# A step rule and a rate for the second instruction stream of a hybrid decoder block

## The chip, the core and the metric

The kernel runs on one core of a Trainium2 chip. The core has a matrix engine (TensorE, PE), a vector engine (VectorE, DVE), a scalar engine (ScalarE, ACT), a general engine (GpSimd, POOL), a queue engine (SyncE, SP) and 16 DMA engines. Each engine takes its instructions from one queue, in the order in which the program was built. The metric is the device time of one execution in microseconds (us), lower being better.

## What is computed

The reference is one decoder block on 1024 tokens of width 1024. Its parts, shortened:

```
h  = x * (1 + scale1) + shift1                     # scale, shift, gate from c (w_ada)
q, k, v, z, xbc, dt, g = split(h @ w_in)
y_attn = diff_attention(q, k, v) @ w_attn_branch   # 8 heads, causal
y_ssd  = mamba2(z, xbc, dt) @ w_ssd_branch         # 32 heads, chunks of 256
mixed  = (sig(g1) * y_attn + sig(g2) * y_ssd) @ w_out
x  = layer_norm(ALPHA * x + gate1 * mixed)
h2 = x * (1 + scale2) + shift2
# PEER, per token: 8 heads pick 16 of 16384 experts each (128 per token)
sc = q_j . sub_keys ; eidx, g = top 16 of the 16 x 16 sums of the best keys
act  = gelu(expert_u[eidx] . h2)
y    = sum(softmax(g) * act * expert_v[eidx])
x  = layer_norm(ALPHA * x + gate2 * y)
```

## The kernel before

**Work.** The tokens are worked in two halves of 512 (`hb` 0 and 1), and each half in four tiles of 128. `main` goes through both halves: attention, the state-space mixer (`ssd`), the output projection with its norm (`post_norm`), and the scores of the expert keys (`scores`). These are the main phases. Then `dense` begins.

**Experts in two ways.** Tiles 1, 2 and 3 are done densely: `dense` goes through all 128 blocks of 128 experts (product `ps_u`, GELU, a table of gates, product `ps_v`). For it, `spread` has to build those tables first: per token a one-hot matrix `first_k` on DVE and one, `second_k`, on POOL, and their product `ps_gate` on PE (128 of each for one tile). Tiles 0 and 4 to 7 are done by gathering (`gathered`): 128 indirect DMAs of 512 KB from `peer_u`, each reduced on DVE (line 1130), then a transposition `ps_wT`, then 128 indirect DMAs from `peer_v`, whose rows PE multiplies with `own` into `ps_y` (a copy on DVE at line 1158 for every four rows). At its end `finish` adds the residual and the last norm (lines 1205 to 1217). Both kinds need `route` first, which finds the experts of a tile on DVE.

**Two streams.** The main stream is `main` and then `dense`. Beside it runs the other stream, of two parts: `side` (the modulation's rest, then the gathers of one tile after another) and `urgent` (the routing of one tile after another, with `spread` where the tile is dense). After each step of the main stream, `drive` adds its cost times `ratio` (`ratio1` in `dense`) to a credit and takes steps of the other stream until it is spent; `step` decides whether a step goes to `side` or `urgent`, by a count and the pair `share` (first number in the main phases, second in `dense`).

**What sets the order on the engines.** A scheduler lays out each engine's queue when the program is built. Instructions of the main stream, and the other stream's matmuls (`inline`), have the same high priority and go by program order among themselves when they are ready by the scheduler's own estimate; the rest of the other stream fills gaps. POOL's instructions of the other stream keep program order. `behind` keeps the other stream on DVE and SP from running ahead of the main stream.

**Buffers that tie the streams.** In the main phases the gathers have four buffers (`n_grow`), ten in `dense`. One bank of PSUM (`gate`) serves `ps_gate`, `ps_wT` and `ps_y`; `claim` hands it over. Four buffers of the tag `row` go round in program order among `scr`, `oh`, `gs`, `ys`, `gy`, the loads of `finish`, and the loads `lnr` of `rows_out`. `rows_out` (lines 991 to 1000), called by `scores`, is the last user of the norm's tiles `v`, whose memory `dense` takes over for `act_t`.

Of the kernel before, what the change touches and what calls it, by code (L numbers as in the profile page):

```python
# [47 lines left out]
class Block:  # L48
# [4 lines left out]

    lead = 2
    ahead = 1000000
    ratio = 0.9
    ratio1 = 1.1

    share = 1, 4
    lag = 6, 2  # L60

    behind_by = 2
# [1325 lines left out]
    def step(self, only=None):  # L1388

        insts = self.nc.cur_bb.bb.instructions  # L1390
        n = len(insts)
        forced = only is not None
        if not forced:
            self.count += 1
            turn = self.count % (1 + self.share[self.dp is not None])
            only = "urgent" if turn == 0 or not self.side else "side"
            if only == "urgent" and (not self.urgent or self.claimed == "side"):
                only = "side"
        order = [only] if forced else [only, "side" if only == "urgent" else "urgent"]
        for which in order:  # L1400
            cost = None
            if which == "urgent" and self.urgent:
                cost = next(self.urgent, None)
                if cost is None:
                    self.urgent = None
            elif which == "side" and self.side:
                cost = next(self.side[0], None)
                if cost is None:
                    self.side.popleft()

            if cost:
                break
        for i in insts[n:]:
            if self.after.get(i.engine):
                self.behind(i, self.after[i.engine])
            if i.engine == mybir.EngineType.Pool:
                if self.pool:
                    self.behind(i, self.pool)
                self.pool = i.name
        return max(cost or 0.0, 0.6)  # L1420
# [123 lines left out]
```

## Time and profile before

| | us |
|---|---|
| three runs | 4841.60, 4845.84, 4854.27; median 4845.84 |
| the profiled execution | 4879.04, span 4877.3 |
| main phases (first half; second half) | to about 1102; to about 2489 |
| entry to `dense` (PE between first and second block) | 2493.9 to 2655.3 |
| `dense` | 2655.3 to about 4445 |
| gathers of tile 7 after it | about 4445 to 4877 |

The profiled execution is 33 us (0.7%) longer than the median of the three runs; differences are worked out in its times. Engines: PE is busy in 82% of the span, DVE in 61%, POOL in 38%, ACT in 29%.

In a row of the timeline the first number is the start and the second the duration, both in us; a bracket gives the time that the engine was idle before, and what ended that. In a row of the windows view a stretch and its length are followed by the busy time of each engine with its count of instructions, then the granted clock of TensorE, the busy share of the DMA engines and their GB/s. A gather's row on POOL is the issuing, not the transfer.

### The profile page before, as it was taken

The page shows a single profiled execution, that of the slowest core. Times are in us where ns is not written, and L with a number is a line of the kernel's source. Part 1 is how long each engine was busy: PE and PEld are TensorE (multiplying, and loading weights), DVE is VectorE, ACT ScalarE, POOL GpSimd, SP SyncE. Part 2 cuts the span into 40 slices and gives each one's busy share as a digit, 9 for nine tenths or more (in the row PEclk, how much of TensorE's full clock was granted, in tenths as well). Part 3 has the DMA queues.
Part 4 walks back from the last instruction along what each step waited for, and adds up shares of the span by engine and source line. Part 5 has one row for each costly group of instructions (what it writes and reads, how often), then busy time and mean ns, then how long its engine had stood idle before and what let it go on. Part 6 is the DMA issues. An engine that isn't in the chain of part 4 may idle for free.

```text
span 4877.3 us, 52557 instructions
## 1 busy us (share of the span) xinstructions
PE 4001.2 (82%) x17996; PEld 2769.0 (57%) x17996; DVE 2976.9 (61%) x6965; ACT 1419.5 (29%) x2340; POOL 1862.1 (38%) x1704
## 2 busy tenths in 40 slices
PE   6999999998888878999975768997799976994045
PEld 4677667786667756755554655556655665552000
DVE  6664646558887896744356994228952399324920
ACT  3544444323453343631112221222222222210000
POOL 1000000001266435333333565445654376445764
PEclk9999999998898988999975989998899989997588
DMA  7323233443356736478744898888988899888998
GB/s 261 121 70 117 76 106 111 146 145 119 95 166 187 245 116 179 115 251 279 257 121 142 325 330 333 298 313 329 370 313 316 313 363 330 309 292 284 395 357 315
DMA packets 441343, 1135.18 MB, mean 233 GB/s; under 512 B 141596, under 2 KB 162228, under 8 KB 441076
## 3 DMA queue, kind: packets, MB, share of 16 engines
q0 software_dynamic: 188704, 677.46, 39.0%
q1 hardware_dynamic: 126644, 405.04, 24.3%
q10 hardware_dynamic: 125728, 49.32, 3.8%
q8 instruction: 143, 2.34, 0.2%
q14 instruction: 124, 1.02, 0.1%
HBM read 1067.56 MB, written 64.11 MB: 232 GB/s over the span
## 4 chain that ended last, share of the span: by engine, by line
PE 52%; DVE 22%; DMA 9%; issue 8%; POOL 6%; ACT 2%; SPq 0%; ACTq 0%; POOLq 0%; DVEq 0%
PE ps_y L1300 9%; DVE grow L1130 7%; PE ps_u L269 7%; PE ps_v L1340 6%; PE ps_b L269 5%; DMA grow<-in_peer_u,ei 4%; PE ps_x L269 4%; DVE wlo L220 3%; PE ps_z L269 3%; PE ps_g L269 3%; POOL grow L1188 3%; PE ps_pq L269 3%; POOL second_k L1272 3%; PE ps_vT L269 2%; PE ps_o L269 2%
## 5 line engine op out<-in xcount | busy, mean ns | idle before, releaser
L1188 POOL DMA_INDIRECT grow<-in_peer_u,ei x640 | 834.0, 1303 | 765.4 <-DVE ei L1233 199.8
L1188 POOL DMA_INDIRECT grow<-in_peer_v,ej x640 | 679.8, 1062 | 766.1 <-PE ps_y L1300 642.4
L219 ACT CAST whi<-wraw 128x1024 fp32r<-128x1024 f32 x498 | 518.1, 1046 | 1228.3 <-PE ps_u L269 401.5
L220 DVE TENSOR_TENSOR wlo<-wraw,whi 128x1024 fp32r<-128x1024 f32 x498 | 606.2, 1219 | 406.2 <-ACT whi L219 361.0
L1130 DVE SCALAR_TENSOR_TENSOR grow<-grow,gh 128x1024 f32<-128x1024 f32 x640 | 766.7, 1218 | 107.7 <-DMA grow<-in_peer_u,ei 104.0
L1300 PE MATMUL ps_y<-grow,own 128*32 128x512 f32 x2560 | 580.7, 620 | 67.8 <-issue 28.7
L1272 POOL TENSOR_SCALAR second_k<-iota_c,at 128x128 f32<-128x128 f32 x384 | 321.7, 847 | 493.0 <-PE ps_gate L1300 303.8
L269 PE MATMUL ps_u<-hhi,wlo 128*128 128x384 f32 x1024 | 383.6, 375 | 138.3 <-DVE wlo L220 138.3
L269 PE MATMUL ps_u<-hhi,whi 128*128 128x384 f32 x1024 | 378.9, 370 | 66.6 <-ACT act_t L1314 52.5
L269 PE MATMUL ps_u<-hlo,whi 128*128 128x384 f32 x1024 | 370.2, 362 | 0.0
L975 POOL DMA_DIRECT2D h2s_d<-bighi x8 | 4.5, 564 | 914.9 <-ACT bighi L245 914.9
L269 PEld LDWEIGHTS ps_u<-hhi,wlo 128*128 128x128 f32 x1024 | 212.4, 207 | 215.2 <-DVE wlo L220 162.5
L1158 DVE COPY own<-wt 128x4 f32<-128x4 f32 x160 | 28.8, 182 | 433.9 <-PE ps_y L1300 342.6
L269 PEld LDWEIGHTS ps_u<-hhi,whi 128*128 128x128 f32 x1024 | 212.6, 208 | 133.6 <-ACT act_t L1314 63.5
L1340 PE MATMUL ps_v<-wlo,ehi 128*128 128x512 f32 x768 | 259.5, 414 | 34.2 <-DVE wlo L220 34.0
L1300 PEld LDWEIGHTS ps_y<-grow,own 128*32 128x32 f32 x2560 | 88.1, 110 | 326.0 <-issue 200.6
L1340 PE MATMUL ps_v<-whi,ehi 128*128 128x512 f32 x768 | 216.8, 405 | 41.6 <-ACT whi L219 38.9
L1340 PE MATMUL ps_v<-whi,elo 128*128 128x512 f32 x768 | 250.7, 404 | 0.0
L1300 PE MATMUL ps_gate<-first_k,second_k 128*128 128x128 f32 x768 | 176.4, 360 | 85.8 <-POOL second_k L1272 59.1
L269 PEld LDWEIGHTS ps_u<-hlo,whi 128*128 128x128 f32 x1024 | 211.8, 207 | 22.4 <-issue 19.3
L1300 PEld LDWEIGHTS ps_gate<-first_k,second_k 128*128 128x128 f32 x768 | 142.3, 246 | 128.9 <-POOL second_k L1272 93.8
L1340 PEld LDWEIGHTS ps_v<-wlo,ehi 128*128 128x128 f32 x768 | 142.0, 193 | 118.6 <-DVE wlo L220 51.2
(340 smaller groups left out, 7996.0 us busy)
## 6 DMA issues: line engine op xcount, KB each, us to landing
wraw<-in_w_in SPq DMA_DIRECT2D x160, 512.0 KB
wraw<-in_peer_uT SPq DMA_DIRECT2D x128, 512.0 KB
wraw<-in_peer_v SPq DMA_DIRECT2D x128, 512.0 KB
wada<-in_w_adaT SPq DMA_DIRECT2D x48, 512.0 KB
g_d<-gs ACTq DMA_DIRECT2D x48, 512.0 KB
gl<-g_d SPq DMA_DIRECT2D x48, 512.0 KB
cr<-cum_d SPq DMA_DIRECT2D x64, 256.0 KB
wraw<-in_w_ssd SPq DMA_DIRECT2D x32, 512.0 KB
```

Of the source, the lines that this page charges most:

```text
L219: nc.scalar.copy(hi, raw)
L220: i = nc.vector.tensor_tensor(lo, raw, hi.bitcast(F32), op=ALU.subtract)
L269: i = self.nc.tensor.matmul(ps, w[x][:, k, :], r[y][:, k, :], start=k + n == 0, stop=k == kk - 1 and n == 2)
L975: nc.gpsimd.dma_start(self.h2s_d[part][:, k, :], big[k][part][:, P * self.few[0] :])
L1130: nc.vector.scalar_tensor_tensor(u, u, 1.0, h2, op0=ALU.mult, op1=ALU.mult, accum_out=act[:, k : k + 1])
L1158: nc.vector.tensor_copy(own[:, :, OWN - 1].rearrange("p (h r) -> p h r", h=2), wt[:, b * n : b * n + n].rearrange("p (h r) -> p h r", h=2) ...
L1188: self.nc.gpsimd.indirect_dma_start(out=r, out_offset=None, in_=table, in_offset=bass.IndirectOffsetOnAxis(ap=ei[:, k : k + 1], axis=0),)
L1272: nc.gpsimd.tensor_scalar(second, self.iota_c, at[:, 1, k : k + 1], None, op0=ALU.is_equal)
L1300: return op(*args, **kw)
L1340: nc.tensor.matmul(acc[2 * tt + c], prev[x][:, tt * P : tt * P + P], v[y].rearrange("p k c -> p (k c)")[:, c * 512 : c * 512 + 512], start ...
```

## The change

Three numbers and one expression. In the main phases the credit grows at 1.25 times the main stream's cost instead of 0.9. There, of every two steps one went to `urgent` and one to `side`; now of three steps two go to `urgent` and one to `side`. In `dense` one step of five goes to `urgent`, before and now, and `ratio1` stays.

```
-    ratio = 0.9
+    ratio = 1.25
     ratio1 = 1.1
 
-    share = 1, 4
+    share = 3, 5
...
-            turn = self.count % (1 + self.share[self.dp is not None])
-            only = "urgent" if turn == 0 or not self.side else "side"
+            turn = self.count % self.share[self.dp is not None] == 0
+            only = "side" if self.side and turn != (self.dp is not None) else "urgent"
```

No instruction is added or removed; the order on the engines changes. PE where `dense` begins, before: `ps_u` is the product of its first blocks, `ps_key` and `ps_gate` belong to the spread of tile 3.

```order
L269 MATMUL ps_u<-hlo,whi 128x384
L269 MATMUL ps_u<-hhi,wlo 128x384
L1300 MATMUL ps_key<-ident,keys 128x128 x2
L1300 MATMUL ps_key<-ident,g 128x128
L1300 MATMUL ps_gate<-first_k,second_k 128x128 x128
L269 MATMUL ps_u<-hhi,whi 128x384
```

Between the first block of `dense` (24 `ps_u`) and the second stand all 128 gate products of tile 3. PE at the same place now:

```order
L269 MATMUL ps_u<-hlo,whi 128x384
L269 MATMUL ps_u<-hhi,wlo 128x384
L1300 MATMUL ps_gate<-first_k,second_k 128x128 x13
L1300 MATMUL ps_wT<-ident,act 128x128
L1300 MATMUL ps_y<-grow,own_101 32x512 x8
L1300 MATMUL ps_y<-grow,own_103 32x512 x8
```

The last row but one and the last alternate, 32 rows of eight, and then the second block follows: of the gate products 13 are left here, and the transposition and all 256 `ps_y` products of tile 0, which stood among the main stream's before, have come here.

POOL around the end of the main phases, before (`peer_v` with `ej` are the second gathers of tile 0; the two loads at line 1009 serve `dense`):

```order
L1272 TENSOR_SCALAR second_k<-iota_c,at 128x128 x68
L1188 DMA grow<-in_peer_v,ej 128x1024 x39
L1009 DMA hlo<-h2s_d_117 128x8x384
L1009 DMA hhi<-h2s_d_116 128x8x384
L1188 DMA grow<-in_peer_v,ej 128x1024 x85
L1272 TENSOR_SCALAR second_k<-iota_c,at 128x128 x128
```

The last 124 of the second gathers stand ahead of the one-hot matrices of tile 3. The same now, up to the first gathers of tile 4:

```order
L1272 TENSOR_SCALAR second_k<-iota_c,at 128x128 x4
L1188 DMA grow<-in_peer_u,ei 128x1024
L1272 TENSOR_SCALAR second_k<-iota_c,at 128x128 x4
L1188 DMA grow<-in_peer_u,ei 128x1024 x3
L1188 DMA grow<-in_peer_v,ej 128x1024 x128
L1188 DMA grow<-in_peer_u,ei 128x1024 x128
```

The one-hot matrices of tile 3 stand among the first gathers of tile 0, four to one, and all 128 second gathers come behind the last of both.

## Rows read from the trace of the kernel before

**Rows 1.** The page: busy times, and one costly group of part 5.

```profile
PE 4001.2 (82%) x17996; PEld 2769.0 (57%) x17996; DVE 2976.9 (61%) x6965; ACT 1419.5 (29%) x2340; POOL 1862.1 (38%) x1704
...
L1130 DVE SCALAR_TENSOR_TENSOR grow<-grow,gh 128x1024 f32<-128x1024 f32 x640 | 766.7, 1218 | 107.7 <-DMA grow<-in_peer_u,ei 104.0
```

**Rows 2.** Windows: PE, PEld, DVE, ACT, POOL busy, in four stretches.

```profile
771.88:1102.50 330.62, 312.21 (x1479) 252.71 (x1478) 180.85 (x360) 113.51 (x168) 8.70 (x16) 0.97 0.44 142
1518.87:2075.90 557.03, 483.96 (x2323) 381.78 (x2322) 427.17 (x972) 251.14 (x396) 240.80 (x244) 0.89 0.56 169
2075.90:2489.10 413.20, 396.77 (x1784) 226.44 (x1783) 177.38 (x496) 88.92 (x125) 134.87 (x127) 0.98 0.76 254
2493.85:2655.30 161.45, 77.58 (x260) 60.01 (x259) 89.78 (x249) 37.70 (x36) 78.11 (x128) 0.51 0.39 105
```

**Rows 3.** Timeline of PE at the entry to dense.

```profile
2493.51 0.34 PE L269 MATMUL ps_u<-hhi,wlo 128*128 128x384 f32 x1
2507.15 0.80 PE L1300 MATMUL ps_key<-ident,keys 128*128 128x128 f32 x2 [13.30 <-DVE keys L1255]
...
2621.34 2.39 PE L1300 MATMUL ps_gate<-first_k,second_k 128*128 128x128 f32 x8 [1.21 <-POOL second_k L1272]
2655.32 0.69 PE L269 MATMUL ps_u<-hhi,whi 128*128 128x384 f32 x1 [31.59 <-ACT act_t L1314]
```

**Rows 4.** Timeline of ACT: what the first GELU of dense waited for.

```profile
2653.48 1.28 ACT L1314 ACT_TABLE_LOAD   x1 [28.61 <-DMA h_d<-v]
```

**Rows 5.** Timeline of DVE: the start of rows_out.

```profile
2622.41 4.71 DVE L991 TENSOR_TENSOR v<-v,lnr 128x1024 f32<-128x1024 f32 x4
```

**Rows 6.** Windows of tile own alone (PE, PEld, DVE, POOL): the gathers' ps_y.

```profile
2075.90:2489.10 413.20, 124.47 (x512) 17.68 (x512) 5.24 (x30) 0.00 (x0) 0.98 0.76 254
```

**Rows 7.** Windows of tile ps_gate alone (PE, PEld, ACT).

```profile
1518.87:2075.90 557.03, 65.69 (x338) 55.30 (x337) 48.44 (x43) 0.89 0.56 169
```

**Rows 8.** Windows of DVE alone: tile oh, then tile val (route of tile 3).

```profile
2040.00:2507.00 467.00, 22.87 (x24) 0.96 0.71 237
2040.00:2507.00 467.00, 22.02 (x137) 0.96 0.71 237
```

**Rows 9.** Timeline of POOL: gathers, six of tile 0 and one of tile 7.

```profile
1183.66 1.05 POOL L1188 DMA_INDIRECT grow<-in_peer_u,ei  x1 [199.82 <-DVE ei L1233]
...
1887.28 1.00 POOL L1188 DMA_INDIRECT grow<-in_peer_u,ei  x1 [0.17 <-issue]
...
2299.16 0.94 POOL L1188 DMA_INDIRECT grow<-in_peer_v,ej  x1 [0.30 <-issue]
2301.68 1.05 POOL L1188 DMA_INDIRECT grow<-in_peer_v,ej  x1 [1.57 <-PE ps_y L1300]
...
2308.66 0.94 POOL L1188 DMA_INDIRECT grow<-in_peer_v,ej  x1 [0.78 <-PE ps_y L1300]
...
2313.43 0.94 POOL L1188 DMA_INDIRECT grow<-in_peer_v,ej  x1 [2.24 <-DMA grow<-in_peer_v,ej]
...
2322.41 0.94 POOL L1188 DMA_INDIRECT grow<-in_peer_v,ej  x1 [2.28 <-DMA grow<-in_peer_v,ej]
...
4662.57 1.13 POOL L1188 DMA_INDIRECT grow<-in_peer_u,ei  x1 [0.30 <-issue]
```

**Rows 10.** Timeline of PE: ps_y of tile 0, then first and last of tile 7.

```profile
2307.32 1.05 PE L1300 MATMUL ps_y<-grow,own 128*32 128x512 f32 x4 [1.06 <-DMA grow<-in_peer_v,ej]
...
2317.86 1.05 PE L1300 MATMUL ps_y<-grow,own 128*32 128x512 f32 x4 [0.84 <-DMA grow<-in_peer_v,ej]
...
4671.51 4.23 PE L1300 MATMUL ps_y<-grow,own 128*32 128x512 f32 x16 [0.56 <-DVE own L1158]
...
4853.79 1.05 PE L1300 MATMUL ps_y<-grow,own 128*32 128x512 f32 x4 [0.20 <-DMA grow<-in_peer_v,ej]
```

**Rows 11.** Timeline of DVE: finish of tile 7.

```profile
4864.93 1.23 DVE L1205 TENSOR_TENSOR gy<-gy,gr 128x1024 f32<-128x1024 f32 x1 [15.51 <-DMA gr<-x_d]
4866.19 1.23 DVE L1210 SCALAR_TENSOR_TENSOR gy<-gr,gy 128x1024 f32<-128x1024 f32 x1
```

## The prediction

> **What bounds the kernel now.** I read the page first: PE is busy in 82% of the span, DVE in 61%, POOL in 38% [rows 1]. That is an average over stages, so next I read the windows by stage. In the last stretch of the second half (gates of the mixer's output, projection, norm, key scores; 2076 to 2489) PE is busy for 396.77 of 413.20 us, or 96%. In the stretch before it, attention's output and the mixer (1519 to 2076), PE is at 87% and DVE at 77%. At the entry to the dense phase, 161.45 us long, no engine is busy for more than 90 us, and the granted clock is 0.51, about the lower of its two levels [rows 2]. The timeline of PE says what this entry is: PE ends the first dense block at 2493.85, waits 13.30 us for the keys of tile 3, does that tile's gate products until 2623.73, and then waits 31.59 us for a GELU [rows 3]. The GELU waited for a write of `v`, the end of `rows_out` [rows 4], which began at 2622.41 [rows 5], when the spread of tile 3 had given back its buffers. So the entry is serial. Whatever of the other stream stands on PE between the first and the second dense block is paid in full there, and `rows_out` is paid after it.
>
> **What moves, part by part.** The new rate and the new share put the one-hot matrices of tile 3 earlier and the first gathers of tile 0 later. The order shows the result. Of 128 gate products of tile 3, 112 go into the last stretch of the main phases and 16 stay behind the last key scores. All 128 second gathers of tile 0 (512 KB each), their 256 `ps_y`, 32 copies on DVE, the write of `y` and `finish` leave that stretch and come to the entry. PE's queue is in order, so the second dense block stands behind all `ps_y`; everything behind it (GELU, DVE's gate multiplication, the loads of further blocks, whose three buffers are full) waits for it.
>
> *The main phases get shorter.* `ps_y` of the gathers leaves: 124.47 us of PE [rows 6]. The gates that come cost 65.69 / 169 = 0.389 us of PE each (338 records are 169 products) [rows 7], and 112 of them 44 us. PE's busy time in the last stretch becomes 396.8 - 124.5 + 44 = 316 us. How full PE is then is not shown. The first half's stretch of the same work, with none of this beside it, has 312.21 of 330.62 (94%), and the stretch with gates has 87% [rows 2]: 336 or 363 us, against 413. I take 350, a gain of 63 (50 to 77). Route 3 moves the other way, into the mixer's stretch, whose DVE is already at 77%: at least 22.87 + 22.02 = 45 us of DVE [rows 8]. From there 34 reductions of the first gathers leave, 34 x 1.22 = 41 us of DVE [rows 1]. These nearly cancel; I take a cost of 10, between 0 and 45. Together -53 us, between -77 and -5.
>
> *The entry gets longer.* Term by term, from the end of the first dense block:
> The rest of the spread and of the first gathers: 16 gates at the pace of the entry before, (2623.73 - 2507.15) / 128 = 0.91 us [rows 3], are 15 us; six first gathers on POOL, some 7 us at one in 1.2 us, lie partly between them. 18 (15 to 22).
> From the last first gather's issue to the first `ps_y`: 4671.51 - 4662.57 = 9 us in tile 7 [rows 9, 10]; nothing hides it.
> The 128 second gathers. With ten buffers tile 7's `ps_y` last from 4671.51 to 4854.84, 183 us or 1.43 each [rows 10]; that is the lower end. Here there are four. One turn of a buffer is issue to product (2307.32 - 2301.68 = 5.64, or 2317.86 - 2313.43 = 4.43), the product 1.05, and release to the next issue (2308.66 - 2308.37 = 0.29) [rows 9, 10]: 5.8 to 7.0 us, and with four in flight 1.44 to 1.75 each. The stretch with four buffers in which PE most often waited for them runs from 2299.16 to 2322.41, twelve gathers, 1.94 each [rows 9], but there PE also had work of its own. I take 1.75, between the turn's long end and that row: 224 us, and 8 for three hand-overs of the one bank, in which four buffers run empty (an estimate, three product waits of 2 to 3 us): 232. The upper end is 1.94 x 128 + 8 = 256.
> From the last `ps_y` to `rows_out`: tile 7 needed 4864.93 - 4854.84 = 10 us to the first multiplication of `finish`, then 2.5 for two of them [rows 11], which release the buffers of `lnr`; its load takes about as long as one of those before it, 5. 18 (13 to 21).
> From the start of `rows_out` to the second dense block: 2655.32 - 2622.41 = 33 [rows 3, 5].
> Sum 18 + 9 + 232 + 18 + 33 = 310 us, where 161.5 were [rows 2]: +148.5, between +92 and +180.
>
> The trace's 4.43 to 5.64 us from issue to product stand against the fit in the Trainium skill, "DMA: Bandwidth & Descriptors", section "Anatomy of one DMA — SWDGE (gpsimd) path", of 2.0 us plus the bytes over 436 GB/s, which makes 3.2 us of one of these gathers; by that the turn is 4.5 us, POOL's issuing at 1.24 us becomes the limit, the second gathers last an estimated 167 us and the sum would be 65 us less. The rows do not agree with it, and I go by them.
>
> *Dense and after it.* Routes 4 to 7 and their gathers start after `rows_out` as before, the step rule there is unchanged, and on PE 288 `ps_y` stand behind the last dense product where 292 did. So the 2222 us from the second dense block to the end (4877.3 - 2655.3) stay.
>
> *Sum:* +148.5 - 53 = +95.5 us on a span of 4877.3. The profiled execution (4879.04) lies 33 us above the median; I carry the difference over unchanged: 4845.84 + 95.5 = 4941 us. From the ends, 92 - 77 = +15 and 180 - 5 = +175, so 4861 to 5021 for this case.
>
> **Rivals.**
> *The early stretches give back more (faster).* The first gathers of tile 0 ran from 1183.66 to 1887.28, 5.5 us each [rows 9]. If the main stream in attention and mixer went at their pace, 34 fewer of them there give back up to 34 x 5.5 = 187 us, and the time is 4941 - 187 = 4754. It decides the sign from 2.8 us a gather. For it: that stretch is much longer than its work on PE. Against it: over all 640 reductions DVE was idle only 104 us for a landing [rows 1], 0.16 us each, so what slows that stretch is mostly the work itself. 8%.
> *The last stretch does not shrink (slower still).* Gates come in pairs of engines (POOL's matrix, PE's product, ACT's copy out of the one bank), and 112 of them with 28 reductions among a main stream that waits in order may hold it at 413 us; route 3 costs its 45. Then +148.5 + 45 = +194, or 5040. For it: the 87% of the stretch with gates. Against it: DVE has 236 us free in that stretch [rows 2]. 12%.
> *It comes to nothing.* The other stream goes at its own pace, not at the credit's; what the entry loses the main phases give back. That needs the second gathers at 1.43 us and the last stretch at its 336 us, the low end: about +15, or, with a little from the first rival, 4846. 7%.
>
> **How the numbers follow.** My case has 73%, the rivals 8, 12 and 7. About 0.3% (15 us) is what a measurement of this kernel can tell from no change. Slower: 71 of my 73, the 12, and 1: 84%. Within: 2 of mine, 4 of the third rival and 1 of the first: 7%. Faster: 7 of the first rival and 2 of the third: 9%. The range takes my case's low end with a little of the third rival, 4856, and reaches to the second rival, 5040.
>
> **What would show it.** In the profile after: between the first and second dense block PE holds `ps_y` of tile 0, about 230 us of it with PE waiting for gathers (the step's size), and the gap there is near 310 us; `rows_out` follows `finish`; the last key scores end 40 to 70 us earlier than 2489; from the second dense block to the end it is 2222 us give or take 15. I am wrong if the gap is under 220 us, if the key scores end later than before, or if the dense phase or the gathers after it change length by more than 30 us.

## The result, and the profile after

The changed kernel took 4916.3 us (median of three runs, 4905.27 to 4919.57), against 4845.84: the ratio is 1.0137, with a 95% interval of 1.0104 to 1.017. It is slower by 1.4%, 70 us, where 95 had been forecast. The medians of the kernel before lay at 4846, 4847, 4868, 4868 and 4852 us in this set and the four that follow, so kernels of different sets are compared below by their ratio to it; 1% is 48 us.

The windows of the kernel after, by stage: start and end, length, then busy time (and count) of PE, PEld, DVE, ACT and POOL, PE's granted clock, the busy share of the 16 DMA engines, and GB/s. The stages are the first half's mixer, the last stretch of the first half, the second half's attention, its output and mixer, its last stretch, the entry, dense, and what comes after the last dense product.

```profile
331.50:784.10 452.60, 421.82 (x1914) 320.00 (x1913) 244.25 (x435) 196.87 (x335) 0.00 (x0) 0.96 0.29 93
784.10:1117.00 332.90, 310.89 (x1473) 251.58 (x1472) 178.76 (x358) 112.22 (x166) 8.69 (x16) 0.97 0.44 140
1117.00:1516.60 399.60, 363.65 (x1648) 252.39 (x1646) 333.07 (x1060) 188.00 (x376) 119.72 (x117) 0.91 0.33 100
1516.60:2042.50 525.90, 469.18 (x2306) 372.14 (x2305) 405.07 (x959) 244.08 (x385) 214.42 (x229) 0.93 0.53 164
2042.50:2400.10 357.60, 309.37 (x1518) 253.13 (x1517) 258.27 (x640) 119.79 (x156) 140.00 (x149) 0.90 0.56 171
2405.00:2704.40 299.40, 152.86 (x540) 25.66 (x538) 46.61 (x104) 9.80 (x13) 134.73 (x146) 0.83 0.82 277
2704.40:4501.50 1797.10, 1547.16 (x6895) 1056.09 (x6895) 1090.48 (x2372) 390.72 (x537) 963.27 (x775) 0.94 0.88 320
4501.50:4914.20 412.70, 134.34 (x513) 19.72 (x513) 194.86 (x382) 3.50 (x7) 281.02 (x250) 0.70 0.93 357
```

Set these beside [rows 2]: the last stretch fell from 413.20 to 357.60 us, the mixer's from 557.03 to 525.90, and the entry grew from 161.45 to 299.40. Read the last two columns as well. In the last stretch before, PE was 96% busy and the DMA engines were at 0.76 and 254 GB/s; after, that stretch has 0.56 and 171 GB/s, and the entry, where PE works half the time, has 0.82 and 277.

The timeline of PE at the entry (start, length, line, operation; in brackets the idle time before it and what ended it), as in [rows 3]:

```profile
2404.62 0.34 PE L269 MATMUL ps_u<-hhi,wlo 128*128 128x384 f32 x1
...
2416.30 1.96 PE L1300 MATMUL ps_gate<-first_k,second_k 128*128 128x128 f32 x6 [0.50 <-POOL second_k L1272]
2429.14 0.48 PE L1300 MATMUL ps_wT<-ident,act 128*128 128x128 f32 x1 [10.88 <-DVE act L1135]
2430.17 4.87 PE L1300 MATMUL ps_y<-grow,own 128*32 128x512 f32 x16 [0.56 <-DVE own L1158]
...
2659.11 1.05 PE L1300 MATMUL ps_y<-grow,own 128*32 128x512 f32 x4 [0.55 <-DMA grow<-in_peer_v,ej]
2704.36 0.69 PE L269 MATMUL ps_u<-hhi,whi 128*128 128x384 f32 x1 [44.20 <-ACT act_t L1314]
```

The wait for keys of [rows 3] is gone. PE ends the first dense block at 2404.96, works through the last gates, and then through all `ps_y` of tile 0, at the pace at which gathers land. Then it waits 44.20 us for the GELU, as it waited 31.59 before. The timeline of POOL shows the gathers at the ends of that stretch, and the first gather of tile 4:

```profile
2420.12 0.94 POOL L1188 DMA_INDIRECT grow<-in_peer_u,ei  x1 [0.30 <-issue]
2421.37 0.94 POOL L1188 DMA_INDIRECT grow<-in_peer_v,ej  x1 [0.31 <-issue]
...
2653.32 0.94 POOL L1188 DMA_INDIRECT grow<-in_peer_v,ej  x1 [0.34 <-PE ps_y L1300]
...
2772.51 1.39 POOL L1188 DMA_INDIRECT grow<-in_peer_u,ei  x1 [118.25 <-DMA gh<-h_d]
```

The timeline of DVE, with `finish` of tile 0 and the start of `rows_out` (compare [rows 5, 11]):

```profile
2670.65 1.22 DVE L1205 TENSOR_TENSOR gy<-gy,gr 128x1024 f32<-128x1024 f32 x1 [24.12 <-DMA gr<-x_d]
...
2677.56 4.63 DVE L991 TENSOR_TENSOR v<-v,lnr 128x1024 f32<-128x1024 f32 x4 [1.42 <-DMA lnr<-in_ln_g]
```

`rows_out` began 17.4 us after the last `ps_y` (2677.56 - 2660.16) and waited for its row, loaded into a buffer that `finish` had held.

### The profile page after: what moved, and what is told of

Same layout as the page of the kernel before. It is cut to its first block, busy times and chain, and to the rows that moved or that the text cites. A ratio compares the mean times of both kernels' runs of the same rounds, so it can differ in the third digit from the quotient of the medians.

```text
span 4914.2 us, 52631 instructions
## 1 busy us (share of the span) xinstructions
PE 3988.6 (81%) x17996; PEld 2749.0 (56%) x17996; DVE 2972.2 (60%) x6965; ACT 1414.7 (29%) x2338; POOL 1879.1 (38%) x1704
## 4 chain that ended last, share of the span: by engine, by line
PE 27%; DVE 14%; DMA 9%; issue 7%; POOL 3%; ACT 1%; ACTq 0%; POOLq 0%; SPq 0%; DVEq 0%
PE ps_u L269 7%; PE ps_v L1340 7%; PE ps_y L1300 7%; DVE grow L1130 6%; DMA grow<-in_peer_v,ej 5%; DMA grow<-in_peer_u,ei 4%; POOL grow L1188 3%; DVE wlo L220 2%; PE ps_pq L269 1%; PE ps_b L269 1%; PE ps_o L269 1%; PE ps_g L269 1%; PE ps_gate L1300 1%; PE ps_z L269 1%; PE ps_x L269 0%
## 5 line engine op out<-in xcount | busy, mean ns | idle before, releaser
L1188 POOL DMA_INDIRECT grow<-in_peer_u,ei x640 | 859.1, 1342 | 734.9 <-DVE ei L1233 199.7
L1188 POOL DMA_INDIRECT grow<-in_peer_v,ej x640 | 659.1, 1030 | 628.5 <-PE ps_y L1300 503.1
L1300 PE MATMUL ps_y<-grow,own 128*32 128x512 f32 x2560 | 611.9, 622 | 117.2 <-DMA grow<-in_peer_v,ej 98.0
L1272 POOL TENSOR_SCALAR second_k<-iota_c,at 128x128 f32<-128x128 f32 x384 | 334.4, 878 | 669.0 <-PE ps_gate L1300 408.1
L269 PEld LDWEIGHTS ps_u<-hlo,whi 128*128 128x128 f32 x1024 | 207.7, 203 | 19.4 <-issue 16.8
L245 ACT CAST ehi<-act_t 128x384 fp32r<-128x384 f32 x128 | 65.7, 513 | 504.6 <-PE ps_v L1340 500.5
L1314 ACT ACTIVATE act_t<-ps_u 128x384 f32<-128x384 f32 x128 | 62.6, 489 | 499.6 <-PE ps_u L269 456.2
```

The source lines that it names most:

```text
L245: nc.scalar.copy(hi, src)
L269: i = self.nc.tensor.matmul(ps, w[x][:, k, :], r[y][:, k, :], start=k + n == 0, stop=k == kk - 1 and n == 2)
L1188: self.nc.gpsimd.indirect_dma_start(out=r, out_offset=None, in_=table, in_offset=bass.IndirectOffsetOnAxis(ap=ei[:, k : k + 1], axis=0),)
L1272: nc.gpsimd.tensor_scalar(second, self.iota_c, at[:, 1, k : k + 1], None, op0=ALU.is_equal)
L1300: return op(*args, **kw)
L1314: nc.scalar.activation(t, ps[:, :n], AF.Gelu)
```

## The experiments

The 13 profiles are best read side by side. "First dense" is the start of the first dense product, "gap" the time between the first and the second dense block, "tile 4" its first gather, and GB/s the mean from the first dense product to the end.

```
run           ratio   95%             first dense  gap    tile 4   span    GB/s
before again  (before)                2490.7       162    2714.1   4858.3  313
after         1.0137  1.0104-1.0170   2399.8       299    2772.5   4914.2  321
ratio         1.0059  1.0037-1.0080   2504.2       165    2729.8   4858.7  314
share         1.0055  1.0034-1.0076   2354.8       310    2743.2   4867.1  322
lnr_after     1.0082  1.0060-1.0103   2396.8       none   2925.7   4869.2  325
cut           0.9790  0.9755-0.9824   2401.6       145    2624.3   4766.9  321
bufs5         1.0006  0.9993-1.0018   2389.3       269    2736.0   4859.8  327
lnr_before    1.0041  1.0029-1.0053   2490.7       184*   2765.2   4889.8  310
lnr_share32   1.0074  1.0043-1.0105   2369.2       none   2893.7   4890.4  319
share_bufs5   0.9987  0.9976-0.9998   2381.0       268    2724.9   4856.4  326
late_rate     1.0089  1.0072-1.0107   2360.6       310    2748.0   4899.9  319
before_bufs5  0.9910  0.9893-0.9928   2485.7       147    2707.5   4817.3  317
lnr_cut       0.9683  0.9663-0.9703   2421.7       none   2667.6   4692.0  330
* after five dense blocks, not one; in the three rows with none, 36, 36 and 21 us stand there
```

**The kernel before, a second profile.** 

> The kernel before, profiled once more, because its first profile lies 33 us above the median of its runs. If that profile was long by chance, its span is now 4840 to 4855 us; the entry to the dense phase is again 161 us and the last key scores end within 15 us of 2489. If the profiler itself lengthens this kernel, the span is again near 4877.

Its span is 4858.3, 19 us shorter than the first profile's; the stages up to the second dense block agree within 3 us (2658.0 against 2655.3), and the difference lies behind it (2200.3 against 2222). So some 20 us of the profile on which the prediction stands were the chance of one execution.

**The rate alone (ratio).** Edit: `ratio = 0.9` to `1.25`, share as before.

> Only the rate 1.25; the shares stay one step in two and one in five. On PE all 128 gate products of tile 3 stand between the first and the second dense block, as before, and no product of the gathers. Theory (what counts is what stands in the entry): entry 150 to 175 us, time 4846 plus or minus 15. Rival (the higher rate itself holds up the main phases): main phases longer by 20 us or more, time 4870 or more.

Slower by 0.6% (0.4 to 0.8). Its windows, first half's mixer, last stretch, entry:

```profile
333.80:786.10 452.30, 423.55 (x1912) 321.28 (x1911) 244.16 (x434) 196.63 (x334) 0.00 (x0) 0.96 0.30 93
...
2078.90:2503.50 424.60, 406.58 (x1821) 230.75 (x1820) 176.85 (x505) 93.60 (x131) 140.94 (x139) 0.98 0.76 250
2508.60:2673.90 165.30, 77.58 (x260) 60.01 (x259) 93.97 (x255) 37.78 (x36) 77.96 (x128) 0.51 0.38 104
```

The median, 4866.6, lies between the theory's time (up to 4861) and the rival's (4870 or more). In the order all second gathers and the entry stay where they were. The last stretch of the first half begins at 786.1 instead of 771.9, as in the changed kernel (784.1), with the same work on PE: the rate holds up the first half, which no term of the sum had. Which wait there it is was not tried.

**The share alone (share).** Edit: the changed kernel with `ratio = 0.9`.

> Only the share, two steps of three to routing and gates, at the old rate 0.9. On PE 25 gate products and all 256 products of tile 0's second gathers stand between the first and the second dense block. Theory: entry about 300 us, as with the whole change, time 4916 plus or minus 20. Rival (it takes both numbers): entry below 220 us, time below 4880.

Windows of the second half's four stages up to dense:

```profile
1103.50:1489.80 386.30, 354.11 (x1647) 247.81 (x1646) 331.33 (x1058) 189.55 (x376) 106.52 (x116) 0.92 0.34 102
1489.80:1995.30 505.50, 458.57 (x2282) 365.86 (x2281) 393.83 (x910) 242.60 (x387) 188.08 (x207) 0.94 0.53 159
1995.30:2355.10 359.80, 309.90 (x1524) 253.66 (x1524) 264.02 (x674) 117.62 (x151) 149.26 (x161) 0.90 0.59 181
2360.70:2670.90 310.20, 156.16 (x562) 30.76 (x560) 52.65 (x120) 12.06 (x15) 147.72 (x158) 0.84 0.83 275
```

The share alone makes the long entry (310 us) and the short last stretch, as expected, but not the expected time: 4872, not 4916. It costs 0.55%, and the rate on top of it the other 0.8%: its main phases end 45 us before those of the changed kernel, 13.5 of it in the first half, 13 in attention and 20 in the mixer.

**Rows of their own for `rows_out` (lnr_after).** The changed kernel, with

```
-                rows.append(self.row("lnr"))
-                nc.sync.dma_start(rows[-1], bcast_rows(src, off, D))
+                rows.append([self.two("lnr") for _ in range(2)])
+                for c, r in enumerate(rows[-1]):
+                    nc.sync.dma_start(r, bcast_rows(src, off + c * 512, 512))
```

and the two multiplications and additions by halves. The rows thus lie in buffers that the main phases use (tag `two`), no longer in the four that the other stream uses as well.

> The changed kernel, with the loads of rows_out in buffers of the main phases (two halves each, tag two) instead of the four row buffers that they share with the other stream. Theory (rows_out, and so the dense phase, waits for finish of tile 0 through those buffers): the entry falls from 299 to under 60 us, the 256 products of the second gathers run among the dense blocks and cost there their 124 us of PE, so the time is 4916 - 260 + 125 = 4780, plus or minus 40. Rival (the dense phase has to wait for the gates or for PE's order in any case): entry above 200 us, time within 20 of 4916.

The wait went: dense products run on from 2396.8, the second block at once behind the first, so it was these buffers that held it. The time fell by only 0.55% (27 us), not by the entry. Windows: tile 0's second gathers beside dense; route 4; the rest of dense; after it.

```profile
2397.00:2810.00 413.00, 393.56 (x1819) 246.27 (x1819) 124.56 (x194) 99.87 (x133) 171.49 (x157) 0.97 0.80 271
2810.00:2925.70 115.70, 108.26 (x536) 93.08 (x536) 98.10 (x323) 40.09 (x54) 0.97 (x2) 1.00 0.59 203
2925.70:4116.00 1190.30, 1026.59 (x4617) 703.26 (x4615) 720.04 (x1493) 261.73 (x359) 667.74 (x534) 0.95 0.90 329
4116.00:4869.20 753.20, 269.07 (x1029) 39.46 (x1027) 378.46 (x851) 7.43 (x14) 542.25 (x491) 0.72 0.96 365
```

PE is at 95% in the first of them, and dense is over 383 us earlier than in the changed kernel (4116.2 against 4498.8). But then 753 us of gathers are left, through which the DMA engines are 96% busy. And POOL issues no gather from 2810.09 to 2925.66:

```profile
2810.09 0.93 POOL L1193 DMA_INDIRECT grow<-in_peer_v,ej  x1 [2.20 <-DMA wraw<-in_peer_v]
2925.66 0.94 POOL L1193 DMA_INDIRECT grow<-in_peer_u,ei  x1 [114.64 <-DVE tkw L1023]
```

What the entry held had gone to the tail. That asked whether the end is set by dense at all.

**A quarter of the gathers at the entry (cut).** The changed kernel with `last = P if tile_no else n` for the loop over second gathers: tile 0 takes 32 of 128 and writes its one block of `y` four times.

> The changed kernel, but tile 0's second gathers stop after 32 of 128 (the block's rows of y are written four times; the other three blocks' sums are left out), so 64 ps_y instead of 256 stand at the entry. Theory (the second gathers with four buffers stand in the entry in full, and everything behind it starts later by as much): the entry shrinks from 299 by 96 x 1.80 = 172 to about 127 us, tile 4's first gather comes at about 2600 instead of 2772, and the time falls by about as much, 4916 - 172 = 4744 us (4725 to 4770). Rival (the entry only delays a stream that has time to spare later): the entry shrinks, but the time falls by less than half of it and stays over 4830.

Ratio 0.979 against 1.0137, 3.5% or 168 us less; the entry became 145 us. Its PE:

```profile
2446.28 1.08 PE L1302 MATMUL ps_y<-grow,own 128*32 128x512 f32 x4 [0.56 <-DVE own L1159]
...
2500.95 1.05 PE L1302 MATMUL ps_y<-grow,own 128*32 128x512 f32 x4 [0.20 <-DMA grow<-in_peer_v,ej]
2552.43 0.69 PE L269 MATMUL ps_u<-hhi,whi 128*128 128x384 f32 x1 [50.42 <-ACT act_t L1316]
```

32 gathers took 55.7 us, 1.74 each, and the entry is paid in full in the time, as the prediction had it.

**Five gather buffers (bufs5).** The changed kernel with `n_grow = 5, 10` and `n_row = 3`.

> The changed kernel with five buffers instead of four for the gathers of the main phases, and three instead of four for the rows. Theory (the pace of the second gathers at the entry is a buffer's turn, 7.2 us measured, over the buffers in flight): 7.2 / 5 = 1.45 us each instead of 1.80 to 1.83, 256 ps_y in about 187 instead of 230 us, entry about 255, time about 4870 (4850 to 4890) if the missing row buffer costs nothing. Rival (POOL's issuing, the hand-over of the one PSUM bank or the memory sets the pace): 1.75 to 1.85 each as with four, no change, 4916 +- 12; or the missing row buffer holds up the main phases by 10 to 40 us and eats the gain.

The ratio is 1.0006, so the change costs nothing any more: 1.3% less, more than the 45 us expected. PE, then POOL:

```profile
2424.43 1.94 PE L1300 MATMUL ps_y<-grow,own 128*32 128x512 f32 x8 [0.56 <-DVE own L1158]
...
2617.15 1.05 PE L1300 MATMUL ps_y<-grow,own 128*32 128x512 f32 x4 [0.21 <-DMA grow<-in_peer_v,ej]
2665.13 0.69 PE L269 MATMUL ps_u<-hhi,whi 128*128 128x384 f32 x1 [46.93 <-ACT act_t L1314]
```

```profile
2415.77 0.94 POOL L1188 DMA_INDIRECT grow<-in_peer_v,ej  x1 [0.30 <-issue]
...
2610.78 0.93 POOL L1188 DMA_INDIRECT grow<-in_peer_v,ej  x1 [0.30 <-PE ps_y L1300]
```

The gathers came at (2610.78 - 2415.77) / 127 = 1.54 us instead of 1.83: four buffers' turn it was (a turn of 7.3 us with four in flight, of 7.7 with five). That gave 30 us at the entry. The rest lies in main phases 10 us shorter and 15 us less behind the entry.

**The kernel before with rows of its own (lnr_before).** The edit of lnr_after in the kernel before.

> The kernel before, with the loads of rows_out in buffers of their own as in lnr_after, so the second dense block need not wait for tile 3's spread. Theory (what ends the kernel is the other stream: the spread of tile 3, routes 4 to 7 and their gathers, which go slower while dense blocks run beside them, so that time taken out of the entry comes back as a longer tail): the entry's 162 us vanish and the last dense product ends about 130 to 200 us earlier than 4448 + 50, but the time falls by no more than 50 us, 4800 to 4860. Rival (the dense products on PE set the end, and the entry is paid one to one): 4847 - 100 or more, under 4750.

Neither came true: four more dense blocks slipped ahead, and PE then met the same serial work, later (PE's timeline, and the window behind these blocks):

```profile
2574.74 0.71 PE L1305 MATMUL ps_key<-ident,keys 128*128 128x128 f32 x2 [39.34 <-DVE keys L1260]
```

```profile
2528.00:2712.00 184.00, 93.24 (x312) 69.10 (x312) 97.81 (x295) 39.73 (x41) 77.96 (x128) 0.54 0.33 85
```

The keys of tile 3 came 68 us later than in [rows 3], tile 4's first gather 51 us later than in the second profile of before, and the time rose by 0.4%. But the other stream was late long before dense began. Tile 0's first second gather, in the kernel before and in this run (POOL):

```profile
1890.76 1.00 POOL L1188 DMA_INDIRECT grow<-in_peer_v,ej  x1 [0.16 <-issue]
```

```profile
1951.76 1.00 POOL L1193 DMA_INDIRECT grow<-in_peer_v,ej  x1 [0.17 <-issue]
```

So 61 of the 68 us had been lost in the main phases, whose buffers the rows now take; where there, was not looked for. What dense blocks let in ahead of the other stream are worth, this run can't show, and it doesn't tell the two theories apart.

**More of the steps for the routes in dense (lnr_share32).** lnr_after with `ratio = 0.9` and `share = 3, 2`.

> The two-of-three share at the old rate 0.9, rows_out's loads in buffers of their own, and in the dense phase every second step instead of every fifth for the other stream's own (urgent) steps, so that route 4 goes on while tile 0's second gathers run. Theory (the end is set by the other stream, whose routes were starved in lnr_after: 115 us without a gather): last key score at about 2355 as in the run with the share alone, no gap on PE, tile 4's first gather at about 2700 or earlier, and a tail after the dense phase well under lnr_after's 753 us; time 4730 to 4830, faster than the kernel before. Rival (second gathers and routes in the dense phase hold each other up, and PE with them): 4850 or more.

The theory fell: 1.0074. Tile 4's gathers began at 2893.7, only 32 us earlier than in lnr_after, and the tail is 762 us (4128.9 to 4890.4).

**Share and five buffers (share_bufs5).** `ratio = 0.9`, `share = 3, 5`, `n_grow = 5, 10`, `n_row = 3`.

> The new share at the old rate of 0.9, with five buffers instead of four for the gathers of the main phases and three instead of four for the rows. Theory (the costs found so far stand beside each other: 45 us for the rate, 45 us for the turn of four buffers at the entry, each seen alone): 4872 - 45 = 4827 us, or 0.5 to 1% under the kernel before on the same chip, with tile 4's first gather at about 2743 - 37 = 2706. Rival (both hold up the same work, so only one of them is had): about 4870, no faster than the share alone.

0.9987: 0.7% or 33 us under the share alone, and level with the kernel before. The savings are not simply added: against bufs5 the rate of 0.9 is worth only 0.2%.

**The rate late (late_rate).** The share with 1.25 only from the key scores of the first half on.

> The new share, with the rate 0.9 until the key scores of the first half and 1.25 from there. Theory (the rate costs 13 us in the first half and some 32 in the second, in different places): last key score of the second half at about 2355 + 32 = 2387, time about 4916 - 13 = 4903 us (4890 to 4915). Rival (the second half is late only because the first half's delay pushes the other stream's work into a worse place): about 4872, as with the share alone.

The time, 1.0089, is between the two. The profile puts the last key score at 2361.0, only 6 us after that of the share alone, not 32: in the second half the rate alone does little to the main phases, and most of the other 32 us came only together with the first half's delay. What else the run lost lies behind the entry (2677.5 to 4899.9, 2222 us, where share has 2196), but that is hardly more than the 22 us by which two profiles of one kernel differ there.

**Five buffers in the kernel before (before_bufs5).** The edit of bufs5 in the kernel before.

> The kernel before, with five buffers for the gathers of the main phases and three for the rows. Theory (the fifth buffer pays only where gathers stand alone with PE waiting for them, and before has no second gather at its entry): no change, ratio 0.997 to 1.003, entry 160 +- 8 us. Rival (a fifth buffer speeds the gathers of the main phases too, and through them the main stream): faster by 20 us or more.

The theory fell, and this is the fastest kernel that computes all: 0.991 (0.9893 to 0.9928). Its PE at the entry:

```profile
2491.55 0.38 PE L1300 MATMUL ps_key<-ident,keys 128*128 128x128 f32 x2
```

The wait of 13.30 us for the keys [rows 3] is gone, since tile 0's second gathers ended 28 us earlier (2420.7 against 2448.96) and the keys are routed behind them: the entry is 147 us. Of the rest against the second profile of before, 5 us lie ahead of the entry and 22 behind it, 2178 us against 2200. Which of the two numbers (buffers, rows) does that was not tried.

**The cut where nothing waits (lnr_cut).** lnr_after with the edit of cut.

> lnr_after with tile 0's second gathers stopped after 32 of 128, as in the run cut (the other three blocks' sums are left out). In lnr_after these gathers lie beside dense products on a PE that does not wait. Theory (from the first dense product to the end the DMA engines set the time: 88 to 96% busy at 320 to 365 GB/s in every kernel so far, so that any bytes taken out of it shorten it): 96 gathers of 0.524 MB are 50 MB, at 325 GB/s 155 us; ratio to the kernel before 1.008 - 0.032 = 0.976 (0.965 to 0.987), though nothing waited for them on PE. Rival (gathers beside dense products are free, and those of after cost only because they stand bare at the entry): under 50 us less, ratio over 0.998.

4.0% or 193 us less than lnr_after, as the theory had it, though these gathers lay beside dense products on a PE 95% busy. They cost there no less than when they stand bare at the entry. The windows from the first dense product to the end, of the kernel before (second profile), the kernel after, lnr_after and lnr_cut:

```profile
2490.70:4858.30 2367.60, 1752.98 (x7693) 1135.95 (x7692) 1368.69 (x2940) 431.00 (x580) 1307.26 (x1152) 0.88 0.86 313
```

```profile
2399.80:4914.20 2514.40, 1839.55 (x7980) 1106.65 (x7978) 1334.80 (x2862) 404.77 (x558) 1380.41 (x1172) 0.89 0.88 321
```

```profile
2396.80:4869.20 2472.40, 1797.67 (x7997) 1082.27 (x7996) 1321.15 (x2859) 409.12 (x560) 1382.44 (x1182) 0.88 0.89 325
```

```profile
2421.70:4692.00 2270.30, 1720.20 (x7591) 1095.12 (x7590) 1312.27 (x2820) 403.48 (x554) 1275.13 (x1075) 0.90 0.90 330
```

Length by GB/s gives 741, 807, 804 and 749 MB: the change put 66 MB more behind the first dense product (128 gathers of 0.524 MB are 67), and the cut took some 50 out (96 of them). The DMA engines are 86 to 90% busy over these 2300 to 2500 us, and in all 13 profiles the mean lies between 310 and 330 GB/s. On the average, then, a gather moved out of the main phases is paid with its bytes at about 0.32 MB a microsecond. But bytes are no exact law here: the 5% between 313 and 330 GB/s are 120 us, and 50 MB at 325 GB/s make 155 of the 193 us. Nor is it shown that the DMA engines set the pace. The windows of the kernel after, over most of tile 4's first gathers and then of its second gathers:

```profile
2780.00:3020.00 240.00, 167.83 (x676) 142.02 (x677) 233.50 (x508) 50.09 (x68) 179.54 (x123) 0.86 0.95 351
3030.00:3320.00 290.00, 286.09 (x1313) 161.80 (x1311) 78.86 (x121) 61.36 (x86) 130.46 (x122) 0.99 0.88 313
```

In the first DVE is 97% busy, in the second PE is 99% busy, with the DMA engines at 0.95 and 0.88.

Another account fits at least as well: the gathers of tiles 4 to 7 are one chain that ends last. In POOL's order they follow one another, and once tile 4's have begun, no two issues lie more than 53 us apart in any profile. From tile 4's first gather to the end ("span" less "tile 4") the ten rows of the table with a gap take 2110 to 2152 us, cut among them with 50 MB less (2166 in the first profile of before). The kernel after began tile 4 58 us later than the second profile of before, and its span is 56 us longer. In lnr_after the chain began 153 us later still and took only 1944 us, because dense was over sooner. The first of tile 6's second gathers and the first gather behind them (POOL), in the kernel after and in lnr_after:

```profile
4193.47 1.99 POOL L1188 DMA_INDIRECT grow<-in_peer_v,ej  x1 [0.30 <-issue]
...
4490.23 0.94 POOL L1188 DMA_INDIRECT grow<-in_peer_u,ei  x1 [1.61 <-PE ps_y L1300]
```

```profile
4291.28 1.76 POOL L1193 DMA_INDIRECT grow<-in_peer_v,ej  x1 [0.30 <-issue]
...
4457.22 0.94 POOL L1193 DMA_INDIRECT grow<-in_peer_u,ei  x1 [0.38 <-issue]
```

That is 297 us beside dense and 166 behind it. In lnr_cut tile 4's gathers began 258 us earlier than in lnr_after, more of the chain went beside dense, and the time fell by 193. So tile 0's second gathers are paid bare at the entry and beside dense products alike, and both times the chain behind them starts later. The runs do not part the DMA engines from PE's order and the buffers as what sets the chain's pace; for that a run with the same bytes and another order of `ps_y` in dense would be needed.

## Why the prediction was right, and where not

The direction, the place and the mechanism of the entry were right: 84% stood on slower, and 4916 lies in the range. The sum was 25 us too high, and it came so near partly by luck, as is shown below.

*The entry*, forecast at 310, measured at 299.4. Term by term: the rest of the spread and of the first gathers 15.2 (2420.12 - 2404.96; forecast 18), the first `ps_y` 10.05 later (9), the second gathers 230.0 (232), then 17.4 to `rows_out` (18) and 26.8 to the second dense block (33). The pace of 1.83 is near the turn that had been read from [rows 9, 10], and bufs5 shows that it is the buffers' turn. By the Trainium skill's fit ("DMA: Bandwidth & Descriptors", "Anatomy of one DMA — SWDGE (gpsimd) path") they would have lasted an estimated 167 us, with four buffers as with five. The runs do not agree: 230 and 194 us were measured, so the rows were the better guide.

*The last stretch*, forecast to give 63, gave 55.6. Its pieces were right: PE busy 309.37 (316 forecast), and 224 gate records, that is 112 products, at 41.33 us (44):

```profile
2042.50:2400.10 357.60, 41.33 (x224) 36.81 (x224) 31.75 (x28) 0.90 0.56 171
```

That makes PE 87% busy there, the lower of the two fills considered, where 350 us had been taken between 336 and 363.

*The step that failed* is "Route 3 moves the other way, into the mixer's stretch ... I take a cost of 10, between 0 and 45". So the last key scores ended 89 us earlier, not 40 to 70. The stretch became 31.1 us shorter, and the attention before it, for which the sum had nothing, 16.8 shorter (399.60 against 416.37). Counted in the traces, of the gathers issued in attention 31 are left of 60, and in the mixer 59 of 72. That is 42 fewer, not 34 from the mixer alone, and 48 us less: 1.1 us net per gather. The first rival's mechanism is thus there, at a fifth of its 5.5 us; its 2.8, from which the sign turns, is far off. The run share shows it larger, with 53 fewer and 82 us, 1.5 each.

*Not priced at all*: the rate's delay of the first half, 14.5 us, which the run ratio shows by itself.

*Dense and after* were to stay at 2222; 2209.8 was measured. But over the kernels with an entry this stretch lies between 2178 and 2222, and 2200 in the second profile of before, so nothing is to be read from 12 us. (The 292 and 288 `ps_y` behind the last dense product are 272 and 266 in the traces, as little apart.)

In sum: -89.0 (14.5 - 16.8 - 31.1 - 55.6) + 138.0 - 12.2 = +36.8 (and 0.1 in the first dense block) between the two profiled spans, against +95.5. The medians differ by 70.5, since the profiled execution of before was 33 us over its median while that of after was at it. "I carry the difference over unchanged" was the second weak step: the terms were 58.6 us too high, and by luck 33.6 of that was undone by it.

*What the prediction did not see* is that a cheaper entry need not be a cheaper kernel. It had the entry as a wait of PE, paid in full; cut bears that out, 154 us of entry for 168 of time. But lnr_after and lnr_cut show that the gathers cost as much with no wait at all. In the kernel before they had gone into a stretch with PE 96% busy and the DMA engines at 254 GB/s [rows 2], ahead of dense. Behind it the gathers of tiles 4 to 7 stand in one chain to the end, and what is put ahead of that chain moves the end, whether PE waits for it or not.

## What to carry to other kernels

When work is moved from one phase to another, look not only at the engine that waits but at the work that ends last, and at what comes to stand ahead of it. Here that was a chain of gathers, and 96 gathers taken out ahead of it gave 168 us where PE waited for them and 193 us where it did not. Taking a wait away can shift the time to the tail, as in lnr_after. The DMA column of both phases deserves a look as well, though these runs do not show that it decides. And take two profiles before a term under 20 us is believed.

## What was not expected

A fifth buffer for gathers, with one row buffer fewer, is worth 0.9% in the kernel before, though at its entry no second gather stands; in the changed kernel it is worth 1.3%. A gather of 512 KB alone at the entry came every 1.83 us with four buffers and every 1.54 with five, 286 and 340 GB/s. The latter is near the 357 and 365 GB/s of the tails behind dense in the changed kernel and lnr_after.
